# Layer 1's input halves over layer 0's score buffers, and the branch to the general search four steps later in the odd layer

## The chip, the cores and the metric

One core of one Trainium2 chip runs the program. The metric is the time of one execution in microseconds; smaller is better. Names of engines: PE multiplies matrices, DVE and POOL work on vectors, ACT does activations and copies with a scale, SP issues the transfers. All five run their own list of instructions in order and wait for each other through semaphores.

## The reference

Two layers over 2048 tokens of width 1024. Layer 0 is an attention over chosen keys beside a convolution, layer 1 a gated short convolution. What matters here, cut from the reference:

```python
def block(args):                                   # 128 queries at a time
    dots = jnp.einsum('bqhd,bsd->bqhs', qib, kif)
    score = jnp.einsum('bqh,bqhs->bqs', wb, jax.nn.relu(dots))
    score = jnp.where(causal[None], score, -jnp.inf)
    _, sel = lax.top_k(score, topk)                # the 256 best keys of a query
    ...                                            # softmax attention over these keys

def odd_layer(h, w_in, conv_w, w_out):
    u = h @ w_in
    b_gate, c_gate, xin, gate = jnp.split(u, 4, axis=-1)
    y = b_gate * causal_depthwise_conv(c_gate * xin, conv_w)
    return (y * jax.nn.silu(gate)) @ w_out

x = x + even_layer(...)      # layer 0: concat(attention * gate, conv * gate) @ w_out
x = x + odd_layer(...)       # layer 1
```

## The kernel before

The tokens are worked on in four chunks of 512 (c = 0 to 3), a chunk in four blocks of 128 rows. The program has two halves.

**The first half** projects all chunks, and for every block scores all keys (`index`, score buffers `sc0` to `sc3` in the pool `scp`), then finds the 256th best score of each row (`select`). `select` makes seven guesses of a threshold: ACT counts by a sign pass over the scores (L793), DVE corrects the guess (L798 to L808). Then DVE picks the best 16 below it (L818 to L832), and writes a mask (L836, to `mb_dr` in memory). This is called the search below. It marks rows where the guess failed in `bad`. The last search is that of blocks 14 and 15, in `sc2` and `sc3`. Beside the searches run the projections of the gates and queries, matmuls into `ps_p`.

**The flag.** After all searches DVE reduces `bad` to `fl` (L983), PE spreads it with a matmul (L985), DVE makes the number `fi` (L987). Each engine then loads `fi` into a register (`TENSOR_LOAD`, L1146) and branches on it (L1147). If it is set, a general search is run instead (`general`, `f_` buffers); it isn't taken with these inputs.

**The second half** starts with `last_gates`, two units of the gate projection of chunk 3, whose inputs `yh`, `yl` are loaded back from memory (L1120, L1121); the tiles are the buffers that hold layer 1's inner result later. `out_even(0)` multiplies chunk 0's `mh`, `ml` by the output weights of layer 0 (four steps), `norm_odd` normalizes, and `odd(0)` does the wide products of layer 1 in 16 steps (8 of `jt`, two yields each) into `ps_w`. A step is 48 matmuls (2 products of `mm3`, 24 each). Into these steps `weave` mixes the convolution of chunk 1 (`cnv`) and the attention of chunk 1 (`att`, 32 units of one block and head): after each step it calls each filler as often as its rate says. `LG = 1` unit of `last_gates` stands ahead of `out_even`, the other beside the norm.

Weights of layer 1 and of the output are used for the first time here: each tile comes in four quarters of 256 KB through `w_stage`, is scaled and split by ACT (L208, L209) and POOL (L210), and is written back for later.

The order in which the instructions stand on each engine is not that of the source. The tile framework plays the program against a time model and puts an instruction where it finds it ready; so a wait that the model sees moves other instructions ahead or behind. Buffers get their place by the order in which pools are opened, and a tile of the second half that lies over one of the first waits until that one's last reader is through.

```python
    weave(even, EX, (cnv, CX))
    drain(even)
    n = norm_odd(x1, acc, late)
    drain(late)
    rv = nc.values_load(fi[0:1, 0:1], min_val=0, max_val=1)
    with tc.If(rv > 0):
```

Of the kernel before, what the change touches and what calls it, by code (L numbers as in the profile page):

```python
# [12 lines left out]
FP32 = mybir.dt.float32  # L13
F16 = mybir.dt.float16
# [7 lines left out]
P = 128  # L22
S = 2048
D = 1024
KD = D // P
NB = S // P
CH = 512
# [15 lines left out]
NCAND = 16  # L43
NWT = 2
LOOK = 2
ATR = 3.5
CE, CX, CN0, CNR, R0, R1, R2 = 1.5, 3.0, 1.0, 1.0, 2.0, 2.0, 2.5
ORDER = ('ggqgqg', 'ggqgqg', 'gggg', 'qq')
EX = 1
TQ, TP = 2, 4  # L50
# [23 lines left out]
def trunk_kernel(ctx: ExitStack, tc: tile.TileContext, xT, pos, wE, woE, wO, woO, par, tab, outT):  # L74
# [48 lines left out]
    def drain(gen):  # L123
        for _ in gen:
            pass

    def weave(main, steps=99, *fills):
        owed = [0.0] * len(fills)
        for n, _ in enumerate(main):
            state["gate"] = state["mm"]  # L130
            for i, (gen, rate) in enumerate(fills):
                owed[i] += rate
                while owed[i] >= 1.0:
                    owed[i] -= 1.0
                    next(gen, None)
            state["gate"] = None
            if n + 1 == steps:
                break
# [286 lines left out]


    with ExitStack() as es:
        csp = es.enter_context(tc.tile_pool(name="csp", bufs=1))
        xp = es.enter_context(tc.tile_pool(name="xp", bufs=2))
        e1 = es.enter_context(tc.tile_pool(name="e1", bufs=2))  # L430
# [1 line left out]
        cvp = es.enter_context(tc.tile_pool(name="cvp", bufs=1))  # L432
        at0 = es.enter_context(tc.tile_pool(name="at0", bufs=2))
        tk = es.enter_context(tc.tile_pool(name="tk", bufs=2))
        scp = es.enter_context(tc.tile_pool(name="scp", bufs=1))
        ps_p = es.enter_context(tc.tile_pool(name="ps_p", bufs=2, space=PSUM))
        ps_i = es.enter_context(tc.tile_pool(name="ps_i", bufs=2, space=PSUM))
        ps_t = es.enter_context(tc.tile_pool(name="ps_t", bufs=1, space=PSUM))
        ps_m = es.enter_context(tc.tile_pool(name="ps_m", bufs=1, space=PSUM))

        cos1 = csp.tile([P, NB, 32], FP32, name="cos1")
        sin1 = csp.tile([P, NB, 32], FP32, name="sin1")
        ki = csp.tile([P, 2, S], F16, name="ki")
        tiny = csp.tile([P, S], FP32, name="tiny")

        def load_x(c, k, t):
            SP.dma_start(out=t, in_=xT[k * P:(k + 1) * P, c * CH:(c + 1) * CH])
# [486 lines left out]
        def rest(c, xs):  # L934
            qs, ch = queries(c, xs), channels(c, xs)
            for unit in ORDER[c]:
                next(qs if unit == "q" else ch)
                yield
            yield from qs
            yield from ch  # L940

        def scan(c, xs):
            qst = project(c, xs)
            select(c, index(c, qst, (0, 1)))
            select(c, index(c, qst, (2, 3)))
# [25 lines left out]
        att = first_attention()  # L971
        weave(r1, NB1, (cn0, CE), (att, ATR))
        scan(3, x3)
        weave(r1, 99, (cn0, CE), (att, ATR))
        state["scanned"] = True
        r2 = rest(2, reload(2))
        weave(r2, 99, (cn0, CE), (att, ATR))
        drain(cn0)
        weave(rest(3, reload(3)), 99, (att, ATR))
        drain(att)  # L980
# [6 lines left out]
        V.tensor_scalar(out=fi, in0=fps[:, 0:1], scalar1=0.5, scalar2=None, op0=ALU.is_gt)  # L987


    mx = ctx.enter_context(tc.tile_pool(name="mx", bufs=1, reuse_waits="tile"))  # L990
    cvp2 = ctx.enter_context(tc.tile_pool(name="cvp2", bufs=1, reuse_waits="tile"))
    l1 = ctx.enter_context(tc.tile_pool(name="l1", bufs=2, reuse_waits="tile"))
# [12 lines left out]
    def attend(c):  # L1005
# [4 lines left out]

        yield from attention(range(c * TT, (c + 1) * TT), tiles, scores, lambda: ps_v.tile([P, 4, 2 * HD], FP32, name="ps_v"), vv, G, LOOK, sink)

# [101 lines left out]
        return l1.tile([P, KD, CH], FP32, name="x1"), l1.tile([P, CH], FP32, name="ssum", bufs=1)  # L1114

    def last_gates():
        xh = l1.tile([P, KD, CH], F16, name="yh", bufs=1)
        xl = l1.tile([P, KD, CH], F16, name="yl", bufs=1)
        for k in range(0, KD, 4):
            SP.dma_start(out=xh[:, k:k + 4, :], in_=xs_dr[NCH - 1][:, 0, k:k + 4])  # L1120
            SP.dma_start(out=xl[:, k:k + 4, :], in_=xs_dr[NCH - 1][:, 1, k:k + 4])  # L1121

        def chan(wt, z):
            ps = ps_w.tile([P, CH], FP32, name="ps_w")
            w = slice(z * P, (z + 1) * P)
            mm3(ps, lambda k: wt[:, 0, k, w], lambda k: wt[:, 1, k, w], lambda k: xh[:, k, :], lambda k: xl[:, k, :])
            return ps

        yield from gates(NCH - 1, GATES[KE:], chan, lambda: l1.tile([P, CH], FP32, name="th1"))

    late = last_gates()
    x1, acc = rows()
    weave(late, LG)
# [4 lines left out]
    cnv = conv(1)  # L1138
# [2 lines left out]
    drain(even)  # L1141
    n = norm_odd(x1, acc, late)
    drain(late)


    rv = nc.values_load(fi[0:1, 0:1], min_val=0, max_val=1)  # L1146
# [44 lines left out]
    for c in range(NCH):  # L1191
        att = attend(c + 1) if c + 1 < NCH else iter(())
        if c > 0:
            cnv = conv(c + 1) if c + 1 < NCH else iter(())
            x1, acc = rows()
            weave(out_even(c, *m[c], x1, acc), 99, (cnv, CNR), (att, R0))
            n = norm_odd(x1, acc, late, (cnv, CNR), (att, R1))
            weave(late, 99, (cnv, CNR), (att, R1))
        yh = l1.tile([P, KD, CH], F16, name="yh", bufs=1)
        yl = l1.tile([P, KD, CH], F16, name="yl", bufs=1)  # L1200
        weave(odd(*n, yh, yl), 99, (cnv, CNR if c else CN0), (att, R1 if c else R2))
        late = out_odd(c, x1, yh, yl, 2 if c + 1 == NCH else 1)
        drain(att)
        drain(cnv)
# [71 lines left out]
```

## Time and profile before

| what | value |
|---|---|
| time, median of 3 runs | 2229.91 us (2226.82 to 2230.98) |
| the profiled execution | 2227.99 us, its span 2226.2 us |
| PE busy | 1990.9 us, 89% of the span |
| DVE busy | 1654.1 us, 74% |
| ACT busy | 1182.8 us, 53% |
| POOL busy | 799.6 us, 36% |
| mean granted clock of PE | 0.970 |

Times in the rows are us from the span's start. An engine's busy time is a mean over stages with different limits; PE is the engine that works in most of them, so the places where PE stands still are where time can be lost or won. The profiled execution took 1.8 us more than its span, and 1.9 us less than the median of the runs.

### The profile page before, as it was taken

How to read it: one execution, taken by the hardware profiler on the slowest of the kernel's cores; microseconds unless marked ns; L12 is line 12 of the kernel's file. 1: busy time of each engine (PE TensorE's matmuls, PEld its weight loads, DVE VectorE, ACT ScalarE, POOL GpSimd, SP SyncE). 2: the span in 40 equal slices, each digit the busy share in tenths (PEclk: the TensorE clock that was granted, in tenths of full speed). 3: DMA queues.
4: the chain of work that ended last, by engine and by line, in shares of the span. 5: the costliest groups of instructions: out<-in, count | busy, mean ns of one | idle time of the engine just before them, and what ended most of it. 6: DMA issues, size and time to landing. Idle time of an engine off the chain costs nothing. (4 is left out here: it accounts for less than half of the span.)

```text
span 2226.2 us, 34966 instructions
## 1 busy us (share of the span) xinstructions
PE 1990.9 (89%) x12252; PEld 1073.4 (48%) x12252; DVE 1654.1 (74%) x3580; ACT 1182.8 (53%) x2411; POOL 799.6 (36%) x761
## 2 busy tenths in 40 slices
PE   5877889888989897798889999999999999999997
PEld 4644464555454543344444444544544444444446
DVE  7999989999987785787875898844899973243224
ACT  5666655567567856367774666632665672121111
POOL 4765343444142402246662544510544551000000
PEclk9889999999999998899999999999999999999999
DMA  6445456334745475668886898853979994334224
GB/s 237 163 160 192 162 175 225 114 119 134 221 131 154 124 229 200 219 181 227 216 212 195 185 214 207 191 144 114 195 169 194 195 192 125 118 108 143 95 100 166
DMA packets 406052, 380.89 MB, mean 171 GB/s; under 512 B 313456, under 2 KB 333680, under 8 KB 385136
## 3 DMA queue, kind: packets, MB, share of 16 engines
q1 hardware_dynamic: 405872, 378.63, 60.9%
q8 instruction: 96, 1.57, 0.3%
q14 instruction: 84, 0.69, 0.1%
HBM read 216.45 MB, written 88.70 MB: 137 GB/s over the span
## 5 line engine op out<-in xcount | busy, mean ns | idle before, releaser
L356 POOL TENSOR_TENSOR pp<-lg,pp 128x512 f16<-128x512 f32 (+3 forms) x320 | 343.0, 1094 | 545.8 <-ACT pp L355 466.1
L187 PE MATMUL ps_w<-nh,wt 128*128 128x512 f16 x1024 | 390.6, 382 | 8.7 <-ACT wt L209 3.1
L188 PE MATMUL ps_w<-nl,wt 128*128 128x512 f16 x1024 | 390.9, 382 | 0.0
L189 PE MATMUL ps_w<-nh,wt 128*128 128x512 f16 x1024 | 388.8, 382 | 0.8 <-POOL wt L210 0.8
L187 PEld LDWEIGHTS <-wt 128*128 128x128 f16 x2112 | 208.4, 99 | 250.2 <-issue 23.4
L188 PEld LDWEIGHTS <-wt 128*128 128x128 f16 x2112 | 208.8, 99 | 245.6 <-issue 29.1
L189 PEld LDWEIGHTS <-wt 128*128 128x128 f16 x2112 | 208.4, 99 | 236.7 <-issue 11.0
L241 DVE SCALAR_TENSOR_TENSOR ps_c<-cin,cwt,ps_c 128x512 f32<-128x512 f32 x348 | 260.3, 748 | 20.7 <-ACT ps_c L239 18.0
L353 ACT ACTIVATE lg<-lg,m 128x512 f32<-128x512 f32 (+3 forms) x320 | 206.9, 648 | 127.6 <-DVE m L346 127.2
L210 POOL TENSOR_TENSOR wt<-w_stage,wt 128x512 f16<-128x512 f32 x136 | 167.4, 1236 | 257.5 <-ACT wt L209 240.9
L187 PE MATMUL ps_p<-xh,wt 128*128 128x512 f16 x480 | 185.8, 388 | 14.0 <-ACT th L222 5.7
L355 ACT CAST pp<-lg 128x512 f16<-128x512 f32 (+3 forms) x320 | 165.3, 548 | 40.1 <-DMA pt<-pp 36.9
L189 PE MATMUL ps_p<-xh,wt 128*128 128x512 f16 x480 | 184.5, 386 | 1.1 <-POOL wt L210 1.1
L188 PE MATMUL ps_p<-xl,wt 128*128 128x512 f16 x480 | 185.4, 386 | 0.0
L738 PE MATMUL ps_i<-ki,qst 128*128 128x512 f16 (+3 forms) x608 | 146.4, 362 | 32.2 <-ACT relu L740 31.8
L379 PE MATMUL ps_v<-vv,pt 128*128 128x64 f16 (+1 forms) x2016 | 125.7, 208 | 54.9 <-DMA pt<-pp 52.8
L740 ACT ACTIVATE relu<-ps_i 128x1024 f32<-128x1024 f32 (+7 forms) x176 | 140.9, 810 | 63.0 <-DVE sc L742 42.7
L742 DVE SCALAR_TENSOR_TENSOR sc<-relu,wi,sc 128x1024 f32<-128x1024 f32 (+7 forms) x140 | 163.7, 1169 | 14.3 <-ACT relu L740 14.1
L187 PE MATMUL ps_p<-wt,xh 128*128 128x256 f16 (+1 forms) x608 | 166.5, 274 | 4.7 <-ACT u L597 2.4
L188 PE MATMUL ps_p<-wt,xh 128*128 128x256 f16 (+1 forms) x608 | 166.5, 274 | 0.6 <-POOL wt L210 0.6
L189 PE MATMUL ps_p<-wt,xl 128*128 128x256 f16 (+1 forms) x608 | 166.1, 274 | 0.8 <-DVE xl L492 0.8
L379 PEld LDWEIGHTS <-pt 128*128 128x128 f16 x2016 | 104.3, 99 | 104.0 <-DMA pt<-pp 74.8
(293 smaller groups left out, 3883.3 us busy)
## 6 DMA issues: line engine op xcount, KB each, us to landing
wt<-w_in_wo_dram SPq DMA_DIRECT2D x48, 1024.0 KB, 4.9
wt<-w_in_we_dram SPq DMA_DIRECT2D x39, 1024.0 KB, 5.5
w_stage<-in_wo_dram SPq DMA_DIRECT2D x64, 256.0 KB, 3.6
w_in_wo_dram<-wt SPq DMA_DIRECT2D x16, 1024.0 KB, 4.9
wt<-w_in_woo_dram SPq DMA_DIRECT2D x16, 1024.0 KB, 4.8
w_in_we_dram<-wt SPq DMA_DIRECT2D x13, 1024.0 KB, 4.8
w_stage<-in_we_dram SPq DMA_DIRECT2D x48, 256.0 KB, 3.5
wt<-w_in_woe_dram SPq DMA_DIRECT2D x12, 1024.0 KB, 4.9
```

What stands on the lines that cost most here:

```text
L187: T.matmul(out=out, lhsT=sh(k), rhs=mh(k), start=k == 0, stop=False)
L188: T.matmul(out=out, lhsT=sh(k), rhs=ml(k), start=False, stop=False)
L189: state["mm"] = T.matmul(out=out, lhsT=sl(k), rhs=mh(k), start=False, stop=k == KD - 1)
L210: G.tensor_tensor(out=wt[:, 1, ks, :], in0=st, in1=wt[:, 0, ks, :], op=ALU.subtract)
L241: ins = V.scalar_tensor_tensor(out=out if t == CK - 1 else acc, in0=ci[:, t:t + CH], scalar=cwt[:, j, t:t + 1], in1=acc, op0=ALU.mult, op1 ...
L353: A.activation(out=e, in_=e, func=AF.Exp, bias=last, scale=-1.0, accum_out=blk["ss"][:, h, si:si + 1])
L355: A.copy(out=pp[:, 0:w], in_=e)
L356: eng.tensor_tensor(out=pp[:, w:2 * w], in0=e, in1=pp[:, 0:w], op=ALU.subtract)
L379: ins = T.matmul(out=av[:, i, 0:w], lhsT=p, rhs=vv[:, kt].rearrange("p a d -> p (a d)")[:, 0:w], start=kt + n == 0, stop=kt == b and n == 1)
L738: T.matmul(out=ps[:, r0:r0 + r], lhsT=qst[:, h, i * P:(i + 1) * P], rhs=ki[:, a, s0 + r0:s0 + r0 + r], start=a == 0, stop=a == 1)
L740: A.activation(out=rl[:, 0:w], in_=ps[:, 0:w], func=AF.Relu)
L742: V.scalar_tensor_tensor(out=sc[:, s0:s0 + w], in0=rl[:, 0:w], scalar=wi[:, b, h:h + 1], in1=tiny[:, s0:s0 + w] if h == 0 else sc[:, s0:s0 ...
```

## The change

The pool of score buffers `scp` is opened first instead of last among layer 0's pools, so that it lies at the bottom of that memory. `yh` and `yl` leave the pool `l1` for a pool of their own, `yp`, which is the first that is opened after layer 0: it lies where the score buffers lay. `mx` (with `mh`, `ml`) comes behind it, over what is left of the score buffers and over `ki`. In the source the first `ALONE = 4` steps of `odd(0)`, with the convolution but without the attention, go ahead of the branch, and the rest goes on behind it; the rate of the attention in `odd(0)` goes from 2.5 to 2.9 a step. Lines of the second half have numbers that are 1 to 7 higher than before.

```diff
+ALONE = 4
-CE, CX, CN0, CNR, R0, R1, R2 = 1.5, 3.0, 1.0, 1.0, 2.0, 2.0, 2.5
+CE, CX, CN0, CNR, R0, R1, R2 = 1.5, 3.0, 1.0, 1.0, 2.0, 2.0, 2.9
...
     with ExitStack() as es:
+        scp = es.enter_context(tc.tile_pool(name="scp", bufs=1))
         csp = es.enter_context(tc.tile_pool(name="csp", bufs=1))
...
         tk = es.enter_context(tc.tile_pool(name="tk", bufs=2))
-        scp = es.enter_context(tc.tile_pool(name="scp", bufs=1))
...
+        ki = csp.tile([P, 2, S], F16, name="ki")
+        tiny = csp.tile([P, S], FP32, name="tiny")
         cos1 = csp.tile([P, NB, 32], FP32, name="cos1")
         sin1 = csp.tile([P, NB, 32], FP32, name="sin1")
-        ki = csp.tile([P, 2, S], F16, name="ki")
-        tiny = csp.tile([P, S], FP32, name="tiny")
...
+    yp = ctx.enter_context(tc.tile_pool(name="yp", bufs=1, reuse_waits="tile"))
     mx = ctx.enter_context(tc.tile_pool(name="mx", bufs=1, reuse_waits="tile"))
...
     def last_gates():
-        xh = l1.tile([P, KD, CH], F16, name="yh", bufs=1)
-        xl = l1.tile([P, KD, CH], F16, name="yl", bufs=1)
+        xh = yp.tile([P, KD, CH], F16, name="yh")
+        xl = yp.tile([P, KD, CH], F16, name="yl")
...
     drain(late)
+    yh = yp.tile([P, KD, CH], F16, name="yh")
+    yl = yp.tile([P, KD, CH], F16, name="yl")
+    main = odd(*n, yh, yl)
+    weave(main, ALONE, (cnv, CN0))


     rv = nc.values_load(fi[0:1, 0:1], min_val=0, max_val=1)
...
-        yh = l1.tile([P, KD, CH], F16, name="yh", bufs=1)
-        yl = l1.tile([P, KD, CH], F16, name="yl", bufs=1)
-        weave(odd(*n, yh, yl), 99, (cnv, CNR if c else CN0), (att, R1 if c else R2))
+            yh = yp.tile([P, KD, CH], F16, name="yh")
+            yl = yp.tile([P, KD, CH], F16, name="yl")
+            main = odd(*n, yh, yl)
+        weave(main, 99, (cnv, CNR if c else CN0), (att, R1 if c else R2))
```

What stands on the engines is shown at three places. First PE, at the branch. Before, the last matmuls of `last_gates` stand ahead of the flag's matmul (`ps_m<-fl`), and the norm (`rs_d`) and the odd layer (`nh`) behind the branch:

```order
L188 MATMUL ps_w<-yl,wt 128x512
L189 LDWEIGHTS wt
L189 MATMUL ps_w<-yh,wt 128x512
L985 MATMUL ps_m<-fl,ones 128x1
L1146 TENSOR_LOAD fi
L1147 COMPARE_AND_BRANCH
L1147 UNCONDITIONAL_BRANCH x2
L169 MATMUL ps_m<-rs_d,ones 128x512
L187 LDWEIGHTS wt
L187 MATMUL ps_w<-nh,wt 128x512
```

In the changed kernel the same place comes right behind the last matmul of layer 0 (`ps_p`):

```order
L190 MATMUL ps_p<-xh,wt 128x512
L986 MATMUL ps_m<-fl,ones 128x1
L188 LDWEIGHTS wt
L188 MATMUL ps_w<-yh,wt 128x512
L188 LDWEIGHTS wt
L188 MATMUL ps_w<-yh,wt 128x512
L1152 TENSOR_LOAD fi
L1153 COMPARE_AND_BRANCH
L1153 UNCONDITIONAL_BRANCH x2
L189 LDWEIGHTS wt
L189 MATMUL ps_w<-yl,wt 128x512
```

So 288 `ps_w` matmuls stood between the end of layer 0 and the branch on PE, and 2 stand there now; the other 286, then the norm and the four lone steps, follow the branch. Behind the norm PE has 240 `ps_w` matmuls ahead of the first score matmul of the attention (`ps_q`), where it had 48; the last attention matmuls of chunk 1 stand 48 `ps_w` matmuls ahead of `out_even(1)`, where it was 144, and from `out_even(1)` on the order is as before but for a few neighbours.

Second DVE, at the end of the last search. Before, rows of the convolution (`ps_c`), of `out_even` (`x`, `ssum`) and of the norm (`rs_`) stand between those of the search:

```order
L241 SCALAR_TENSOR_TENSOR ps_c<-cin,cwt,ps_c 128x512
L179 TENSOR_TENSOR ssum<-ssum,sq 128x512
L832 SCALAR_TENSOR_TENSOR t_pick,t_Tn<-tab_sb,t_j_7876,t_cand 128x17
L836 TENSOR_SCALAR mb<-sc_7564,t_T 128x2048
L241 SCALAR_TENSOR_TENSOR ps_c<-cin,cwt,ps_c 128x512
L838 TENSOR_TENSOR t_Tn<-t_T,t_Tn 128x2
L241 SCALAR_TENSOR_TENSOR ps_c<-cin,cwt,ps_c 128x512
L839 SCALAR_TENSOR_TENSOR t_Tn<-t_j,t_Tn 128x2
```

In the changed kernel the search has DVE to itself up to the branch:

```order
L833 SCALAR_TENSOR_TENSOR t_pick,t_Tn<-tab_sb,t_j_7876,t_cand 128x17
L837 TENSOR_SCALAR mb<-sc_7564,t_T 128x2048
L839 TENSOR_TENSOR t_Tn<-t_T,t_Tn 128x2
L840 SCALAR_TENSOR_TENSOR t_Tn<-t_j,t_Tn 128x2
L841 SCALAR_TENSOR_TENSOR bad<-t_j,t_Tn 128x2
L984 TENSOR_REDUCE fl<-bad 128x1
L988 TENSOR_SCALAR fi<-ps_m 128x1
L1152 TENSOR_LOAD fi
```

From the last threshold on, 23 rows of the convolution, 8 of `x` and 7 of `ssum` moved from between these rows to behind the branch.

Third SP, in the changed kernel. The loads of `yh`, `yl`, `mh` and `ml` stand behind the stores of the last two masks, which wait for DVE:

```order
L838 DMA mb_dr_128<-mb 128x1920
L838 DMA mb_dr_129<-mb 128x2048
L1122 DMA yh<-xs_dr_143 128x2048
L1123 DMA yl<-xs_dr_143 128x2048
L1137 DMA mh<-mc_dr 128x2048
L1137 DMA ml<-mc_dr 128x2048
L1152 TENSOR_LOAD fi
L1153 COMPARE_AND_BRANCH
```

Before, `mh` and `ml` were loaded ahead of the last projections, and `yh` and `yl` ahead of the last quarters of the first `out_even` weights, both long ahead of these two stores.

## Rows read from the trace of the kernel before

**Rows 1.** The page, part 1: busy us, share of the span, instructions.

```profile
PE 1990.9 (89%) x12252; PEld 1073.4 (48%) x12252; DVE 1654.1 (74%) x3580; ACT 1182.8 (53%) x2411; POOL 799.6 (36%) x761
```

**Rows 2.** Busy time in a stretch: PE, PEld, DVE, ACT, POOL; granted clock, DMA share, GB/s.

```profile
850.00:860.00 10.00, 2.74 (x7) 0.90 (x8) 3.19 (x20) 6.73 (x9) 2.40 (x3) 0.50 0.85 278
```

**Rows 3.** PE in order of time, where layer 0 ends.

```profile
844.45 0.38 PE L189 MATMUL ps_p<-xh,wt 128*128 128x512 f16 x1
856.10 1.01 PE L187 MATMUL ps_w<-yh,wt 128*128 128x512 f16 x2 [11.27 <-DMA yh<-xs_dr]
858.27 0.58 PE L188 MATMUL ps_w<-yl,wt 128*128 128x512 f16 x1 [1.16 <-DMA yl<-xs_dr]
```

**Rows 4.** ACT in order of time, the search's last counts.

```profile
855.99 2.00 ACT L793 ACTIVATE junk<-sc,t_x 128x2048 bf16<-128x2048 f32 x1
861.47 0.63 ACT L208 ACTIVATE w_stage<-w_stage 128x512 f32<-128x512 f32 x1 [3.39 <-DMA w_stage<-in_woe_dram]
862.65 1.89 ACT L793 ACTIVATE junk<-sc,t_x 128x1920 bf16<-128x1920 f32 x1
```

**Rows 5.** DVE in order of time: last thresholds, last picks and mask, `fl`.

```profile
859.68 0.16 DVE L808 TENSOR_TENSOR t_x<-t_x,t_g 128x2 f32<-128x2 f32 x1
868.75 0.16 DVE L808 TENSOR_TENSOR t_x<-t_x,t_g 128x2 f32<-128x2 f32 x1
889.76 1.21 DVE L823 SCALAR_TENSOR_TENSOR mk<-mb,sc 128x1024 f32<-128x1024 bf16 x1
900.47 2.18 DVE L823 SCALAR_TENSOR_TENSOR mk<-mb,sc 128x1024 f32<-128x1024 bf16 x1
921.25 1.27 DVE L836 TENSOR_SCALAR mb<-sc,t_T 128x2048 bf16<-128x2048 f32 x1
925.93 0.16 DVE L983 TENSOR_REDUCE fl<-bad 128x1 f32<-128x16 f32 x1
```

**Rows 6.** DVE's stretch from last threshold to `fl`: all; L241, L1030, L179 alone.

```profile
868.90:926.10 57.20, 54.71 (x255) 24.55 (x253) 53.24 (x88) 25.33 (x43) 19.53 (x16) 1.00 0.57 195
868.90:926.10 57.20, 16.40 (x23) 1.00 0.57 195
868.90:926.10 57.20, 5.44 (x8) 1.00 0.57 195
868.90:926.10 57.20, 5.44 (x7) 0.00 (x0) 1.00 0.57 195
```

**Rows 7.** SP in order of time: issues of `yh` and `yl`.

```profile
850.56 0.42 SPq L1120 DMA_DIRECT2D yh<-xs_dr  x1
851.03 0.42 SPq L1121 DMA_DIRECT2D yl<-xs_dr  x1
```

**Rows 8.** The branch (register loads, compare), and the rows behind it.

```profile
L1146 PEldq TENSOR_LOAD <-fi x1: 1467/1467/1467, 929.4 to 929.4; - x1
L1147 PEldq COMPARE_BRANCH  x1: 228/228/228, 930.9 to 930.9; - x1
934.26 0.42 DVE L149 SCALAR_TENSOR_TENSOR rs_r<-rs_t,rs_r 128x4 f32<-128x4 f32 x1 [4.81 <-DVEq L1147]
936.53 2.05 PE L169 MATMUL ps_m<-rs_d,ones 128*128 128x512 f32 x2 [9.94 <-DVE rs_d L163]
```

**Rows 9.** The norm's sums on PE, and where DVE takes them up.

```profile
921.32 1.02 PE L158 MATMUL ps_m<-ones,ssum 128*128 128x1 f32 x8
926.72 0.15 DVE L160 TENSOR_SCALAR rs_a<-ps_m 128x4 f32<-128x4 f32 x1
```

**Rows 10.** Busy time by stage, columns as in rows 2.

```profile
858.27:925.38 67.11, 65.33 (x294) 28.89 (x293) 55.42 (x104) 30.97 (x50) 19.97 (x17) 0.97 0.59 203
925.38:940.07 14.69, 2.41 (x5) 0.95 (x5) 7.31 (x21) 3.62 (x7) 3.24 (x3) 0.68 0.70 235
940.07:1190.35 250.28, 223.70 (x1340) 108.72 (x1340) 188.06 (x356) 176.13 (x394) 141.08 (x128) 0.97 0.80 210
```

**Rows 11.** PE's waits from 940.07 to 1190.35: us, times, longest.

```profile
PE ps_v L379 <- DMA pt<-pp: 16.8, 16, 2.5
```

## Prediction

> **What bounds the kernel now.** I read the page's busy shares first: PE works 1990.9 us of the span [rows 1], so the time is PE's work plus the places where PE stands still, and the change leaves the work alone. Then I read the order of the changed kernel against that of before, which shows that both agree up to the end of layer 0 and again from `out_even(1)` on. So only the stretch between is to be priced, and I went through it in the trace: the busy time in slices of 10 us for PE's holes, the timeline of PE, ACT, DVE and SP around them, and the busy time by stage.
>
> Layer 0 ends on PE at 844.83 (the last `ps_p` row, 844.45 + 0.38) [rows 3]. Then PE stands 11.27 us until `yh` has landed, starts a pair at 856.10, and goes on with `yl` from 858.27 [rows 3]. The slices show this hole (2.74 us of work in 850 to 860 [rows 2]) and a second one from 925.38 to 940.07, where PE is busy for 2.41 us of 14.69 [rows 10]: there the flag, the branch and the norm follow each other. Between the two lie 67.11 us in which PE is busy for 65.33 [rows 10].
>
> What the reader is to see is what runs beside these 67 us. The last search is far from over when layer 0 ends: its seventh count on ACT begins at 862.65 [rows 4], its threshold is there at 868.91, its last mask at 922.52 and `fl` at 926.09 [rows 5]. All this is late, but it costs little, because PE has the two gate units and `out_even(0)` to do meanwhile, and the flag is asked for only when they are done.
>
> **The change part by part.**
>
> *The layout takes that cover away.* In the changed order the flag's matmul stands on PE right behind the last `ps_p`. PE works in order, so it stands still until the search has written `fl`. The loads of `yh` and `yl` stand on SP behind the store of the last mask, since their place was the score buffers', so PE's next matmuls wait for the search too. So the restart of PE is now: end of the search, then transfer, then branch.
>
> When does the search end? Up to the threshold the order is nearly the same. Before, ACT's seventh count waits behind a weight quarter that comes 3.39 us late [rows 4]; it was issued after the 2 MB of `yh` and `yl` and lands behind them, and in the changed order these come later. That can bring the threshold 2.9 us forward (the sixth pair of counts ends at 858.0 and its threshold is there at 859.84 [rows 4, 5]; two more counts of 1.9 and 2.0 and their read-outs, some 4.3, and 1.8 again for DVE give 866.0) or nothing (868.9). I take 866.9, nearer to the first, since the cause of the wait moves away.
>
> Behind the threshold DVE was busy 53.24 us up to `fl`, of which 16.40 are the convolution, 5.44 are `x` and 5.44 `ssum` [rows 6]; these 38 rows (23, 8 and 7) now stand behind the branch. What is left is 53.24 - 27.28 = 25.96. One row of it took 2.18 us, where the same kind took 1.21 at 889.76 [rows 5], while POOL was splitting weights; POOL's list is empty there in the changed order, so 25.0. `fl` comes at 866.9 + 25.0 = 891.9, and the last mask 1.0 earlier (between the two lie 3.57 us before, of which four convolution rows fill some 2.6) [rows 5, 6]: 890.9.
>
> Then the transfer. SP issues the mask's store first and `yh` behind it; one issue follows the other by 0.47 us [rows 7], so `yh` goes out at 891.4 and `yl` at 891.9. From issue to PE's first pair took 856.10 - 850.56 = 5.54 us, from `yl`'s issue to its matmul 7.24 [rows 3, 7]. So the pair runs from 896.9 to 897.9; the register load takes 1.47 and the compare 0.23 [rows 8]: 899.6, and `yl` is there at 891.9 + 7.24 = 899.1. PE is back at work at 899.7 where it was at 858.27: **+41.4**. The bounds are 39.5 (quick threshold, transfers 1.5 us shorter since no weights run beside them) and 44.6 (threshold at 868.9, one more us in the transfer).
>
> By the Trainium skill (Runtime: NRT & Kernel Launch, section Instruction fetch mechanics) a taken branch to a place outside the page that was fetched ahead costs a fetch before the engine goes on. The trace shows DVE, which jumps over the general search, idle for 4.81 us at the branch [rows 8], and doesn't show PE's share, since PE waits there for DVE's norm. If PE paid DVE's price the sum would be 3.1 us higher; I go by PE's own two rows, as it has nothing to jump over.
>
> *The 286 matmuls.* They took 67.11 us, of which PE was idle for 1.78 [rows 10]. The first ones after the hole ran at the lower of the clock's two levels, granted 0.50 from 850 to 860 [rows 2]: that stays, since PE comes out of a hole again. DVE now has no search beside them: **-1.0** (from -1.8, all of that idle time, to +2, if the weight quarters that SP issues behind the loads of `kk` and `vv` come late).
>
> *The norm.* From the last `yh` matmul to the first of the odd layer were 14.69 us [rows 10]. In it DVE's chain waits 4.81 us at the branch [rows 8], and begins late besides: the sums of the norm were ready on PE at 922.34, but DVE took them at 926.72 [rows 9], behind the convolution and the search. In the changed kernel neither is there. What remains is eleven small rows, the diagonal, the matmul of 2.05 us [rows 8], and the first row of `nh`: some 9.5 us, estimated from 14.69 less 4.81 and less the late start that PE didn't cover, of which the 16 matmuls behind the sums in the new order cover 3.5 (65.33 us for 294 rows [rows 10]). I take 6.0 and so -8.7, and another -1.0 for less time at the lower clock after a shorter hole: **-9.7** (bounds -12 and -5).
>
> *The odd layer.* PE's work from 940.07 to 1190.35 is unchanged: 223.70 us busy of 250.28 [rows 10]. Before, the 32 attention units lay in 13 steps, now in 11, behind five lone steps instead of one, and one to three lone steps fewer at the end. Of the 26.6 us of idle time 16.8 are waits for the attention's transposed weights [rows 11]. They come per unit, and the units are the same, with less other work between them; the transfers, busy 0.80 of the stage [rows 10], have 18% more to do in the mixed steps. **+3** (bounds: -8, half of these waits go because the convolution is ahead by then; +14, they nearly double). The higher rate itself costs nothing else: 12 x 2.9 = 34.8 calls are enough for 32 units and the closing one.
>
> *The sum*: 41.4 - 1.0 - 9.7 + 3.0 = **+33.7 us**. The profiled execution took 2227.99, so it would be 2261.7; the median of the runs is 1.9 above it, so I forecast 2229.9 + 33.7 = **2264** (rounded). The four lone steps stand ahead of the branch in the source alone; the order has them behind it, and they cost nothing but what the odd layer's term says.
>
> **The rivals.**
>
> *The odd layer gives more back.* If the waits for transposed weights (16.8 us [rows 11]) vanish, since the attention begins when the convolution has most of its rows behind it, the odd layer gives -17 instead of +3: 2229.9 + 41.4 - 1.0 - 9.7 - 17 = 2244. Against it: the units come closer together, not farther apart.
>
> *The denser attention costs more.* The waits double, and the last unit ends just ahead of `out_even(1)`: +18 instead of +3, 2279. For it: the share of transfers is high in that stage. Against it: there are still 48 matmuls, some 10.5 us, between the last attention matmul and `out_even(1)`.
>
> *Faster: the search is over in time.* Then PE would restart at 858.3 plus the 1.7 of the branch, and the norm's gain would stay: 2229.9 + 1.7 - 1.0 - 9.7 + 3.0 = 2224. The point from which it decides: PE must be back by 858.3 + 7.7 = 866.0, so `fl` must be there by some 858. But at 862.65 the seventh count only begins [rows 4], and 25 us of DVE's work follow it. I see nothing in the order that shortens this by 30 us.
>
> *No change*: the hole is there, but layer 0's end moves back by as much because the score buffers lie elsewhere. Nothing in the trace shows a dependence on where buffers lie.
>
> **How the numbers follow.** My forecast has a chance of 0.78, the first rival 0.09, the second 0.08, the third 0.03, no change 0.02. A difference under 0.2% (4.5 us) is about what a measurement of this kernel can't tell from no change. So faster 0.03, same 0.02, slower 0.95. The range: the low bounds of all four terms add to 39.5 - 1.8 - 12 - 8 = 17.7, the high ones to 44.6 + 2 - 5 + 14 = 55.6; that all fall to one side is unlikely, and I go about halfway from the forecast to each end and a little farther, to the slower rival: +18 to +50, 2248 to 2280. That leaves the first rival out, and the second just in.
>
> **What would show it.** After: PE without a matmul from 844.8 to some 897, in one hole of about 52 us, whose end is put down to `yh`'s transfer or the flag; `fl` near 892 and no convolution row on DVE between the last threshold and `fl`; PE's bulk of `ps_w` from about 900; the first `nh` matmul near 974 instead of 940, without a branch in the norm; `out_even(1)` near 1227, and from there all as before, 34 us later. I am wrong if `fl` comes before 875, if PE has matmuls between 845 and the flag, or if the stage from the first `nh` matmul to `out_even(1)` is shorter than 240 us.

## The result, and the profile after

The changed kernel takes 2303.21 us (median of 4 runs, 2300.32 to 2308.68), the kernel before 2228.36 (4 runs, 2225.91 to 2230.98). The ratio is 1.0336, 95% interval 1.0317 to 1.0355: slower by 74.9 us, where +33.7 was forecast. The sign was right; the time lies above the range.

The page, part 1 of the kernel after, beside [rows 1]: PE is busy 11 us longer with the same 12252 matmuls, at a mean granted clock of 0.955 instead of 0.970, so most of the 75 us is idle time.

```profile
PE 2002.0 (87%) x12252; PEld 1075.6 (47%) x12252; DVE 1660.8 (72%) x3580; ACT 1182.5 (51%) x2411; POOL 799.4 (35%) x761
```

Busy time in stretches, after (columns as in rows 2): three slices inside the hole, then the stages that answer to [rows 10]: the `ps_w` work up to the norm, the norm, the odd layer.

```profile
850.00:860.00 10.00, 0.00 (x0) 0.00 (x0) 1.62 (x10) 7.98 (x13) 3.42 (x3) 0.59 0.41 131
880.00:890.00 10.00, 0.00 (x0) 0.00 (x0) 9.83 (x17) 0.00 (x0) 0.00 (x0) 0.50 0.00 0
900.00:910.00 10.00, 4.11 (x11) 1.60 (x12) 0.16 (x1) 0.00 (x0) 0.00 (x0) 0.50 1.01 303
...
907.46:976.36 68.90, 66.84 (x294) 28.81 (x293) 31.37 (x50) 24.09 (x42) 17.90 (x16) 0.96 0.62 222
976.36:983.97 7.61, 1.10 (x3) 0.40 (x4) 2.81 (x6) 1.79 (x4) 0.52 (x1) 0.84 0.84 267
983.97:1265.41 281.44, 231.27 (x1340) 112.02 (x1340) 194.63 (x359) 178.91 (x401) 143.01 (x130) 0.92 0.69 188
```

The hole is what was forecast: no PE, then DVE alone with the search, then the transfer. The surprise is the last row. The same 1340 PE rows as in [rows 10] take 281.44 us instead of 250.28. Of these 31.2 us, 7.6 are PE's own rows, which run at a granted clock of 0.92 on the mean instead of 0.97, and 23.6 are waits.

PE in order of time, after, at the hole (compare [rows 3]) and at the end of the odd stage:

```profile
847.53 0.38 PE L190 MATMUL ps_p<-xh,wt 128*128 128x512 f16 x1
900.00 0.56 PE L986 MATMUL ps_m<-fl,ones 128*128 128x1 f32 x2 [52.10 <-DVE fl L984]
905.61 1.01 PE L188 MATMUL ps_w<-yh,wt 128*128 128x512 f16 x2 [5.05 <-DMA yh<-xs_dr]
907.46 0.59 PE L189 MATMUL ps_w<-yl,wt 128*128 128x512 f16 x1 [0.84 <-DMA yl<-xs_dr]
...
1252.14 0.82 PE L380 MATMUL ps_v<-vv,pt 128*128 128x128 f16 x8 [3.79 <-DMA pt<-pp]
1259.39 0.82 PE L380 MATMUL ps_v<-vv,pt 128*128 128x128 f16 x8 [5.31 <-DMA pt<-pp]
1262.87 1.11 PE L404 MATMUL ps_m<-id,a_nat 128*128 128x128 f32 x4 [1.65 <-DVE a_nat L400]
1265.41 1.01 PE L188 MATMUL ps_w<-mh,wt 128*128 128x512 f16 x2 [1.43 <-ACT mh L183]
```

The last four rows are the attention's last units and then `out_even(1)` at once: no `nh` matmul lies between them, so every wait of that chain is PE's. I call this a flush end. The waits at it, with two shorter ones between these rows, add to 12.7 us. The same place before:

```profile
1172.84 0.60 PE L403 MATMUL ps_m<-id,a_nat 128*128 128x128 f32 x4
1190.35 0.38 PE L187 MATMUL ps_w<-mh,wt 128*128 128x512 f16 x1
```

Between these two rows of before stand 68 `nh` and `nl` matmuls. So the section on the change is wrong where it counts 48 matmuls behind the attention now and 144 before: they are none and 68. The stretch of the flush end, after, as busy time:

```profile
1248.40:1265.41 17.01, 4.40 (x36) 3.29 (x37) 4.55 (x12) 4.62 (x11) 2.26 (x2) 0.58 0.70 188
```

PE's waits from 983.97 to 1265.41, after (us, times, longest; first three lines), to be held against [rows 11], and the waits for `wt` before, from 940.07 to 1190.35 (last two):

```profile
PE ps_w L188 <- ACT wt L210: 22.9, 10, 5.3
PE ps_v L380 <- DMA pt<-pp: 17.8, 13, 5.3
PE ps_w L190 <- POOL wt L211: 3.7, 5, 2.2
...
PE ps_w L187 <- ACT wt L209: 3.1, 3, 1.6
PE ps_w L189 <- POOL wt L210: 0.8, 3, 0.4
```

The waits for staged weights (`wt`) grew from 3.9 to 26.6 us. Those for transposed weights (`pt`) hardly changed in sum, but moved: 9.6 of the 17.8 us lie behind 1248.40, at the flush end, and 8.2 in all the rest of the stage.

All points together, each from the rows above and [rows 3, 10]:

| point on PE | before | after | later by |
|---|---|---|---|
| last `ps_p` ends | 844.83 | 847.91 | 3.1 |
| `ps_w` goes on with `yl` | 858.27 | 907.46 | 49.2 |
| first `nh` matmul | 940.07 | 983.97 | 43.9 |
| first `mh` matmul of `out_even(1)` | 1190.35 | 1265.41 | 75.1 |
| end of the span | 2226.2 | 2301.1 | 74.9 |

From `out_even(1)` on nothing more is lost.

### The profile page after: what moved, and what is told of

It reads as the page before. It is cut to its first block, busy times and chain, and to the rows that moved or that the text cites. A ratio compares the mean times of both kernels' runs of the same rounds, so it can differ in the third digit from the quotient of the medians.

```text
span 2301.1 us, 34969 instructions
## 1 busy us (share of the span) xinstructions
PE 2002.0 (87%) x12252; PEld 1075.6 (47%) x12252; DVE 1660.8 (72%) x3580; ACT 1182.5 (51%) x2411; POOL 799.4 (35%) x761
## 5 line engine op out<-in xcount | busy, mean ns | idle before, releaser
L242 DVE SCALAR_TENSOR_TENSOR ps_c<-cin,cwt,ps_c 128x512 f32<-128x512 f32 x348 | 261.3, 751 | 24.2 <-ACT ps_c L240 20.4
L188 PE MATMUL ps_p<-xh,wt 128*128 128x512 f16 x480 | 185.6, 387 | 15.1 <-ACT th L223 5.5
L794 ACT ACTIVATE junk<-sc,t_x 128x640 bf16<-128x640 f32 (+5 forms) x84 | 118.6, 1412 | 69.2 <-DVE t_x L809 42.1
```

What stands on the lines that cost most here:

```text
L188: T.matmul(out=out, lhsT=sh(k), rhs=mh(k), start=k == 0, stop=False)
L242: ins = V.scalar_tensor_tensor(out=out if t == CK - 1 else acc, in0=ci[:, t:t + CH], scalar=cwt[:, j, t:t + 1], in1=acc, op0=ALU.mult, op1 ...
```

## The experiments

Theory at the start: the layout makes PE wait for the search (some 44 us), and the four lone steps with the rate 2.9 cost the rest in the odd layer. Rivals: the layout costs there too, through late loads; or the closer packing alone; or the flush end alone. Below, "odd stage" is the time from PE's first `nh` matmul to the first `mh` matmul of `out_even(1)`.

**The layout alone** (`e1_layout`)

Against the changed kernel:

```diff
-CE, CX, CN0, CNR, R0, R1, R2 = 1.5, 3.0, 1.0, 1.0, 2.0, 2.0, 2.9
+CE, CX, CN0, CNR, R0, R1, R2 = 1.5, 3.0, 1.0, 1.0, 2.0, 2.0, 2.5
...
-    weave(main, ALONE, (cnv, CN0))
```

> The layout alone: the score buffers first, yh and yl in their own pool over them, but no lone steps, attention rate 2.5 as before. Theory (the layout makes the hole, the lone steps and the rate make the odd layer dear): the first nh matmul stays near 984 (44 us later than before) and the odd stage takes about 250 us again, so 2228 + 44 = 2272 (2266 to 2279). Rival (the odd layer's loss comes from the layout too, because the loads of kk, vv and the weight quarters are issued late, behind the branch on SP): odd stage about 280, time near 2303.

Measured: 2279.76 us, ratio 1.0222 (1.0197 to 1.0247). First `nh` matmul at 983.81, odd stage 255.14. The hole is the layout's, and the odd layer is nearly as before; the time is 0.8 us above the range, with 4.9 us lost in the odd stage.

**The steps alone** (`e2_steps`: the layout of before, `ALONE = 4`, rate 2.9)

> The four lone steps and the rate 2.9 alone, with the layout of before. Theory: PE has no hole but the two of before (first nh matmul near 940), and the odd stage takes some 281 us as in the changed kernel, so 2228 + 31 = 2259 (2252 to 2266). Rival (the loss in the odd stage follows from the layout): odd stage near 250, time 2228 (2224 to 2234).

Measured: 2261.56, ratio 1.0141 (1.0120 to 1.0162); first `nh` matmul at 941.93, odd stage 278.45. So the odd layer's loss belongs to the steps and the rate, but for some 5 us. By the times the two parts cost 49 and 31 us apart, and 75 together.

**A covered end** (`e7_after_r36`: the changed kernel, `R2 = 3.6`)

> The changed kernel with an attention rate of 3.6 in place of 2.9: the attention ends 68 nh matmuls (some 15 us) ahead of out_even(1) instead of flush with it, and is packed closer. Theory of two causes (weight quarters late in the mixed steps 22.7 us, uncovered end 12.7 us): the end's 12 us go, the waits for weights in the mixed steps stay or grow a little, so 2303 - 12 + 4 = 2295 (2288 to 2302). Rival (the density of the attention is all of it): packed closer it gets worse, 2303 to 2315.

Measured: 2281.03, ratio 1.0237 (1.0217 to 1.0257); odd stage 259.04. Faster than even the theory had it. PE's waits there, same columns:

```profile
PE ps_v L380 <- DMA pt<-pp: 17.8, 13, 3.4
PE ps_w L188 <- ACT wt L210: 6.4, 6, 2.0
PE ps_w L190 <- POOL wt L211: 1.2, 6, 0.3
```

Packed closer, the attention costs less: with the flush end 19.0 us of the 26.6 us of waits for `wt` go as well. That packing closer is what costs is refuted. The end has 68 matmuls behind it again, as before the change, and 22.4 of the 31.2 us are gone; 8.8 us are left.

**The pool for `yh`, `yl` over the index keys** (`e5_scplast`: the changed kernel with `scp` opened last, as before)

> The changed kernel with the score pool opened last again, as before, so that the pool of yh and yl lies over the index keys ki and the array tiny, which are free since the last scoring; lone steps and rate as changed. Theory (PE stands still because the place of yh and yl is read until the search ends): yh and yl are loaded ahead of the end of layer 0, the hole of 52 us is gone, and the one of 11 us of before too; the odd stage stays at some 281. 2228 - 11 + 31 = 2248 (2240 to 2258). Rival (a pool of their own, or the flag ahead of the gates, makes the hole): time near 2300.

Measured: 2259.61, ratio 1.0136 (1.0114 to 1.0157); odd stage 282.12. PE in order of time:

```profile
849.27 0.38 PE L190 MATMUL ps_p<-xh,wt 128*128 128x512 f16 x1
849.49 0.38 PE L188 MATMUL ps_w<-yh,wt 128*128 128x512 f16 x1
...
927.73 0.39 PE L986 MATMUL ps_m<-fl,ones 128*128 128x1 f32 x2 [1.31 <-DVE rs_t L149]
934.57 2.05 PE L170 MATMUL ps_m<-rs_d,ones 128*128 128x512 f32 x2 [6.45 <-DVE rs_d L164]
938.10 1.01 PE L188 MATMUL ps_w<-nh,wt 128*128 128x512 f16 x2 [1.49 <-ACT nh L183]
```

No hole at all: the place of `yh` was the cause. With it the order changed back too, for the flag's matmul stands behind the gates again. The time is 1.6 us above the range, since the first `nh` matmul comes only 2 us sooner than before. The 11 us at the end of layer 0 [rows 3] were hidden behind DVE, whose search sets the flag and the norm at 927 either way.

**The flush end alone** (`l2_r25`, `l2_r27`: the steps alone with `ALONE = 2`, `R2 = 2.5` and `2.7`)

> The layout of before, two lone steps in place of four, attention rate 2.5 as before: so the units are packed no closer than before, but the attention of chunk 1 again ends right ahead of out_even(1), without nh matmuls behind it. Theory (an attention that ends flush with out_even(1) is what costs): odd stage some 270, 2231 + 20 = 2251 (2244 to 2258). Rival (the number of lone steps and the closer packing cost): at most a third of the 28 us of four lone steps, 2231 to 2240.

> As the last one, with rate 2.7: the attention ends 36 nh matmuls (some 8 us) ahead of out_even(1). Theory (the flush end costs): most of it goes, 2231 + 7 = 2238 (2232 to 2244). Rival (closer packing costs): as slow as with rate 2.5 or slower.

Measured: 2245.17, ratio 1.0071 (1.0053 to 1.0089), odd stage 264.96; and 2237.17, ratio 1.0035 (1.0021 to 1.0049), odd stage 256.91. The higher rate with 36 matmuls of cover is the faster one, as the theory says. But the flush end costs 8 us here, not the 20 that I had put down for it: covered, the two lone steps still cost 6.6 us of the stage.

**The rate alone** (`e3_rate`: before with `R2 = 2.9`)

> The kernel before with the attention rate 2.9 in place of 2.5, nothing else: the attention starts at the same place and ends 144 nh matmuls ahead of out_even(1) instead of 68. Theory (packing closer costs little as long as the end is covered): odd stage 250 to 258, time 2228 to 2237. Rival (the higher rate is what costs): odd stage over 265, time over 2243.

Measured: 2234.79, ratio 1.0016 (1.0004 to 1.0028), odd stage 255.05 in the profiled execution, which at 2243.53 is the slowest of the ten. The rate is nearly free.

**No staging of weights** (`n1_after`, `n2_before`: the odd layer computes with other weights, already prepared ones)

```diff
-            wt = weight(wp, stg, wO, 2 * jt)
+            wt = weight(wp, stg, wE, T_K)
...
-            wt = weight(wp, stg, wO, 2 * jt + 1)
+            wt = weight(wp, stg, wE, T_K)
```

> The changed kernel with the staging of the odd layer's weights left out: every tile of w_in of layer 1 is replaced by one already prepared tile of layer 0, one transfer, no scaling and splitting on ACT and POOL (the computed values are other ones). Theory of two causes: PE's waits for wt (26.6 us) go but for a few, those at the end for pt stay, so odd stage 281 - 24 = 257 and 2303 - 24 = 2279 (2270 to 2285). Rival (the waits for wt are only where a late attention shows first, and move to pt): odd stage over 270, time over 2290.

> The kernel before with the staging of the odd layer's weights left out in the same way (one prepared tile of layer 0 instead of each tile of w_in of layer 1; the computed values are other ones). With the changed kernel this leaving out took the odd stage from 281 to 234 us. Theory (the loss in the odd stage is the flush end, some 11 us, and a staging that is later among the attention, some 20): without staging the two kernels differ by the end alone, odd stage here 222 to 226. Rival (the lone steps cost something besides staging and end): 215 or less; or (the staging accounts for nothing of the difference): some 203.

Measured: 2251.68, ratio 1.0099 (1.0082 to 1.0117), and 2197.64, ratio 0.9852 (0.9831 to 0.9873; two runs); the odd stage 234.06 and 219.76. Both are below what I expected: I had counted only the waits for `wt`, and in both kernels more goes (PE's waits for `pt` fall too, from 17.8 to 13.5 and from 16.8 to 4.9 us). The first `nh` matmul comes at 979.29 instead of 983.97, and the stage gains in the rest too. The difference between the two kernels shrinks from 31.2 to 14.3 us. In these lie the flush end (in `n1_after` 7.2 us for `pt`, 1.65 and 1.43 behind it) and what the lone steps cost otherwise.

**A third staging buffer** (`k1_third_after`, `k2_third_before`, `k3_third_noconv`). What is late can be seen in the changed kernel; SP and PE in order of time. The first row is quarter one of a tile, the second quarters two and three, the third quarter four:

```profile
1099.79 0.34 SPq L204 DMA_DIRECT2D w_stage<-in_wo_dram  x1
1110.09 0.90 SPq L204 DMA_DIRECT2D w_stage<-in_wo_dram  x2
1118.10 0.33 SPq L204 DMA_DIRECT2D w_stage<-in_wo_dram  x1
...
1106.69 0.38 PE L188 MATMUL ps_w<-nh,wt 128*128 128x512 f16 x1
1116.89 0.61 PE L188 MATMUL ps_w<-nh,wt 128*128 128x512 f16 x1 [5.25 <-ACT wt L210]
```

PE takes up the tile at 1106.69 and waits 5.25 us inside it for a quarter that SP issued at 1110.09, behind transposes; the last quarter is issued 11.4 us after PE began. Two buffers carry all quarters, and each is free only when POOL has split it among the attention's rows.

```diff
-    stg = ctx.enter_context(tc.tile_pool(name="stg", bufs=2))
+    stg = ctx.enter_context(tc.tile_pool(name="stg", bufs=3))
```

(For the room, `lg` has 7 buffers in place of 8, and `t_cand` and `t_parts` one in place of two.)

> The changed kernel with a third w_stage buffer (and, for the room, 7 in place of 8 lg buffers, one in place of two t_cand and t_parts). Theory (in the odd stage the four quarters of a weight tile go through two staging buffers, which POOL frees late among the attention's work, so that the last quarter is issued up to 12 us after PE has begun with the tile): PE's waits for wt fall from 26.6 to under 10 us, the waits at the flush end stay, odd stage 281 to some 262. In the time 2303 - 19 = 2284 (2272 to 2292), less whatever the buffer gives layer 0. Rival (the quarters are late because of their place on SP behind the transposes, or because POOL is slow, which a buffer doesn't mend): odd stage over 274.

> The kernel before with the same third w_stage buffer. Theory: PE's waits for wt are 3.9 us there, so the odd stage gains little, 243 to 252 instead of 250; layer 0, whose weights pass through the same buffers, may gain some us: time 2215 to 2230. Rival (7 lg buffers or the other order of layer 0 cost): over 2232.

Measured: `k1` 2264.77, ratio 1.0158 (1.0134 to 1.0182), odd stage 248.99; `k2` 2237.82, ratio 1.0041 (1.0026 to 1.0056), odd stage 242.55. SP and PE in order of time for the same tile in `k1`, its fourth quarter the first of the pair at 1082.94:

```profile
1082.94 1.00 SPq L204 DMA_DIRECT2D w_stage<-in_wo_dram  x2
...
1093.64 0.38 PE L188 MATMUL ps_w<-nh,wt 128*128 128x512 f16 x1
...
1221.96 1.72 PE L380 MATMUL ps_v<-vv,pt 128*128 128x128 f16 x16 [5.59 <-DMA pt<-pp]
```

The last quarter is now issued 10.7 us ahead of PE, PE has no wait for `wt` in the stage at all, and the stage is 32.5 us shorter in the changed kernel against 7.7 in the one before. Of the 32.5 us, 10.2 are PE's own rows (231.27 to 221.10 us busy, at a granted clock of 0.96 instead of 0.92). The flush end's wait for `pt` stays. What is left between the two kernels is 6.4 us. So the two buffers held the quarters back, and not their place on SP's list alone. The times show less (`k1` still lies below its range, `k2` above), since layer 0 ends at 871 to 873 there instead of 845 to 848.

The Trainium skill (Perfetto Trace Analysis, section Optimization Strategy) says that the same gap repeating on the engine that should be saturated can mean there is no room for the next tile, by the number of buffers. The waits for `wt` are such gaps (15 in this stage), and the third buffer removed them all.

**What points to a faster version** (`c4_flaglate`, `h1_noconv`, `h2_noconv_flaglate`, `m2_third_layer1`, `m4_third_yp`)

`c4_flaglate` moves the lines from `fl` to `fi` behind the norm of the kernel before:

> The kernel before, where only the reduction to fl, its matmul and fi are written behind the norm, directly ahead of the branch, so that the branch stands 48 matmuls behind the norm on PE and not ahead of it. Theory (the branch costs the norm 4.81 us on DVE): first nh matmul at 935 instead of 940, and nothing new behind it, 2231 - 5 = 2226 (2221 to 2230). Rival (the norm waits for DVE, which is busy with the search up to the same time): 2229 to 2233.

Measured: 2237.94, ratio 1.0037 (1.0019 to 1.0054). The first `nh` matmul is at 935.12, as expected, but the odd stage takes 261.28, with 15.1 us of waits for `wt`. More than the gain was given back, and the time is above both ranges; why the staging is later there stays open.

`h1_noconv` has `yp` over the index keys, no lone steps, and

```diff
-CE, CX, CN0, CNR, R0, R1, R2 = 1.5, 3.0, 1.0, 1.0, 2.0, 2.0, 2.5
+CE, CX, CN0, CNR, R0, R1, R2 = 1.5, 0.0, 1.25, 1.0, 2.0, 2.0, 2.5
```

`h2_noconv_flaglate` adds the later flag, `k3_third_noconv` the third buffer.

> A version that takes up what the runs showed: yh and yl in their own pool over the index keys (loaded early, no hole at the end of layer 0), no lone steps, rate 2.5, and the convolution of chunk 1 not in out_even(0) but all in the odd layer (rate 1.25), so that DVE has the last search without its 23 rows. Theory (with the hole gone DVE's search sets the time of the branch and the norm): fl near 908 instead of 926, first nh matmul near 932 instead of 940, odd stage 250 to 258, time 2228 - 8 + 4 = 2224 (2216 to 2230). Rival (the convolution's rows are only moved into a stage that is as full): odd stage 262 or more, 2232 or more.

> As the last one, with the flag and the branch written behind the norm, so that PE doesn't stop for fl inside out_even(0) and the branch stands 48 matmuls behind the norm. Theory: PE works through from 849 to the norm, first nh matmul near 922; the odd stage, in which the branch now lies, 258 to 264; time 2228 - 18 + 11 = 2221 (2213 to 2228). Rival (the later branch gives all of it back, as far as 9 us were given back without the other changes): 2230 or more.

> The version without the convolution in out_even(0), which took 2220.8 us, with the third w_stage buffer. Its attention now ends 57 nh matmuls ahead of out_even(1) but the convolution's last rows stand behind the last units. Theory (weights wait less: 10 us of waits for wt were left in the odd stage): odd stage 246 to 254, time 2206 to 2221. Rival (no gain, since PE waits for the convolution or pt instead): 2221 or more.

Measured: `h1` 2220.83, ratio 0.9957 (0.9942 to 0.9972), `fl` at 905.30, first `nh` matmul at 926.55, odd stage 254.14. `h2` 2229.73, ratio 0.9998 (0.9986 to 1.0010), first `nh` matmul at 923.56, odd stage 262.39: here the later branch gives it back again. `k3` 2230.27, ratio 1.0011 (0.9998 to 1.0023), odd stage 245.25, but layer 0 ends at 873 and the time is above the range.

`m2_third_layer1` gives the second half a staging pool of its own; `m4_third_yp` adds `yp` over the index keys:

```diff
-    stg = ctx.enter_context(tc.tile_pool(name="stg", bufs=2))
...
     with ExitStack() as es:
+        stg = es.enter_context(tc.tile_pool(name="stg", bufs=2))
...
+    stg = ctx.enter_context(tc.tile_pool(name="stg2", bufs=3, reuse_waits="tile"))
```

`t_cand` and `t_parts` have two buffers again here; `lg` has 7.

> The kernel before with the third w_stage buffer in the second half alone (a staging pool of its own there, two buffers in layer 0 as before; 7 in place of 8 lg buffers). With the buffer everywhere the odd stage took 243 us, but layer 0's last ps_p came at 873 instead of 845 and half of it was made good up to the norm. Theory (the later end of layer 0 comes from staging in layer 0 that runs ahead): last ps_p near 846, first nh matmul near 940, odd stage 242 to 250: 2228 - 6 = 2222 (2215 to 2229). Rival (the later end of layer 0 comes from weights of the second half that are staged early, ahead of layer 0's last work): last ps_p near 870 again, 2235 or more.

> As the last one, and yh and yl in their own pool over the index keys, opened as in the version that took 2220.8 us, but with the convolution in out_even(0) as before. Theory: no hole at the end of layer 0, the norm bound by DVE's search at 935 to 940, odd stage 242 to 250: 2220 (2212 to 2228). Rival (as above): last ps_p near 870, 2230 or more.

Measured: `m2` 2217.49, ratio 0.9946 (0.9925 to 0.9968), and `m4` 2218.06, ratio 0.9943 (0.9927 to 0.9958), both faster than before by 12 us. Busy time of `m2` in its odd stage, to be held against [rows 10]:

```profile
936.32:1174.50 238.18, 223.23 (x1341) 110.89 (x1341) 194.03 (x356) 173.82 (x396) 142.51 (x128) 0.96 0.85 228
```

Layer 0 ends at 849.51, so its late end came with what `k1` and `k2` had changed in layer 0: the third buffer there, or the single buffers of `t_cand` and `t_parts`. No run separates the two. The odd stage of `m2` is 12.1 us shorter than before with the same work of PE, in the fastest of its six executions; that of `m4` is 8.3 us shorter. So even the kernel before lost time to its staging, though its own waits for `wt` were only 3.9 us: in `m2` these are gone, and the waits for `pt` fall from 16.8 to 11.8 us as well.

## Why the prediction was right in direction and wrong in size

The terms of the sum, as the prediction has them, against the points in the traces:

| term | forecast | measured | how |
|---|---|---|---|
| end of layer 0 | 0 | +3.1 | 844.83 to 847.91 |
| layout: PE's stop | +41.4 | +46.1 | 13.44 to 59.55 us from there to `yl` |
| the 286 matmuls | -1.0 | +1.8 | 67.11 to 68.90 |
| the norm | -9.7 | -7.1 | 14.69 to 7.61 |
| the odd layer | +3.0 | +31.2 | 250.28 to 281.44 |
| sum | +33.7 | +75.1 | span: +74.9 |

**The layout**: the mechanism held step by step, but the term lies above its bounds. One step of the sum was mis-sized, the search without its neighbours. DVE in order of time, after, from the last threshold to `fl`, and then a convolution row and its follower before:

```profile
870.86 0.16 DVE L809 TENSOR_TENSOR t_x<-t_x,t_g 128x2 f32<-128x2 f32 x1
871.05 2.21 DVE L819 TENSOR_SCALAR_CACHE_REDUCE mb<-sc,t_x 128x1920 bf16<-128x1920 f32 x1
...
899.69 0.17 DVE L984 TENSOR_REDUCE fl<-bad 128x1 f32<-128x16 f32 x1
...
878.13 0.76 DVE L241 SCALAR_TENSOR_TENSOR ps_c<-cin,cwt,ps_c 128x512 f32<-128x512 f32 x1
878.79 1.22 DVE L751 MAX8 t_parts<-mk 128x8 f32<-128x1024 f32 x1
```

It took 28.84 us (871.02 to 899.86, 28.21 of them busy), where I had 25.0 by taking the other rows' busy time from the whole. That takes off too much. Before, all but one of those rows overlap the next: the convolution row at 878.13 lasts 0.76 us, and the next starts 0.66 us after it. The 37 of them that stand ahead of `fl` last 27.2 us added up, but fill only 24.2 us of DVE's time. With that the step comes out at 53.2 - 24.2 = 29.0, less the 1.0 for the stretched row 28.0, close to the 28.2 measured. The threshold came at 871.02, 23.1 us behind the end of layer 0, where before it came 24.1 behind it: the quicker end of the search that I had at 2.0 was 1.0. The way from `fl` to `yl` took 7.6 us (899.86 to 907.46), where I had 7.8. (Worked over from its own rows, the term's bounds would have been 39.0 and 44.4, not 39.5 and 44.6.) The forecast of the hole and of the branch's place on PE was right.

**The norm** lost its branch, and its 14.69 us fell to 7.61, not to the 5.0 of the term. ACT in order of time, after, shows what is late next:

```profile
982.78 0.63 ACT L209 ACTIVATE w_stage<-w_stage 128x512 f32<-128x512 f32 x1 [5.79 <-DMA w_stage<-in_wo_dram]
983.32 0.60 ACT L183 CAST nh<-xi 128x512 f16<-128x512 f32 x1
```

The first `nh` stands on ACT behind the scaling of a weight quarter that has not landed. Without staging (`n1_after`) the first `nh` matmul came 4.7 us sooner. My estimate left out what stands ahead of `nh` on its own engine.

**The odd layer** is the step that failed: +3 (bounds -8 and +14), measured +31.2. Two sentences of the prediction were wrong. "There are still 48 matmuls, some 10.5 us, between the last attention matmul and `out_even(1)`" was misread from the order: there are none, as the rows at 1252 to 1265 show. The prediction's own count says so too: 33 calls of the attention are needed, `weave` makes them after each of the 12 steps that are left, and 11 x 2.9 = 31.9, so the last two calls stand behind the last step (and the units lie in 12 steps, not in 11). And I named the waits for transposed weights (`pt`) as what might change, whereas those for staged weights, 3.9 us before and put at nothing in the sum, grew to 26.6.

How much each cause has can't be told as two shares. Without staging the change costs the stage 14.3 us instead of 31.2, with the third buffer 6.4, with the end covered (`e7_after_r36`) 8.8. So either cure takes away more than half, 16.9 to 24.8 us, and most of the waits for `wt` go with the covered end too: as far as these runs show, the late staging and the flush end cost this much only together. Why an attention that ends early leaves the staging in better order is argued, not shown: the steps behind its end have nothing else on ACT, POOL and SP. What is left with the end covered, 8.8 us, stays open in part: 4.6 of it are PE's own rows (228.29 us busy instead of 223.70).

**The rivals**: "the denser attention costs more" had the right sign and place, and half of its mechanism: the last unit does end right ahead of `out_even(1)`, and I argued that down with the wrong sentence above. The other half, the packing, is refuted (`e7_after_r36`, `e3_rate`). That the odd layer gives something back was wrong, and faster and no change were rightly unlikely. The statement that the first `nh` matmul would come near 974 had the odd layer's +3 in it; the three terms ahead of it give 970.8. And the range's lower end does not lie about halfway from the forecast, as the prediction says: +18 is the sum of all low bounds, 17.7.

**The branch on PE**: by the Trainium skill (Runtime: NRT & Kernel Launch, section Instruction fetch mechanics) a taken branch to a place that was not fetched ahead stalls the engine. In `h1_noconv` the branch lies among PE's matmuls: PE goes from one to the next in 0.30 us (908.69 to 908.99) where 0.22 is usual, while DVE, which jumps over the general search, is idle for 4.72 us, of which 3.9 lie between its compare (909.5) and what comes next (913.5). DVE's pause agrees with the rule, though no run shows that it is a fetch; PE's agrees with the prediction, which gave it nothing to jump over.

## What to carry to other kernels

A tile that is laid over a buffer waits for its last reader. If that reader is the end of a long chain on another engine, the tile belongs over something that dies earlier; the same pool over the index keys had no hole. Work that is woven into a stage should end with cover behind it: count the bulk matmuls between its last one and the reader of its result, and read that count off the order twice. And an engine's small waits before a change (here 3.9 us for staged weights) say little about how close its supply runs; the time from the last issue to the first use shows it. In the kernel before, the last quarter of the same tile as above, the tenth of sixteen, was issued only 0.8 us ahead of PE (SP and PE in order of time), and with the third buffer 10.7:

```profile
1076.20 0.33 SPq L203 DMA_DIRECT2D w_stage<-in_wo_dram  x1
...
1076.98 0.38 PE L187 MATMUL ps_w<-nh,wt 128*128 128x512 f16 x1
```

## What the runs showed that I had not expected

Rows of DVE that stand among other work can't be priced by subtracting their durations. Before, all but one of the 37 rows beside the search ended some 0.08 us after their follower had begun, 3.0 us in all; that is most of what the search's step was too short by.

The third staging buffer, with the smaller tiles that made room for it, moved layer 0's end 23 to 28 us back where it held for the whole program (847.91 to 871.11 and 844.83 to 873.00), and the same buffer in the second half alone gained 12 us. What helps one stage of a kernel can cost more in another.
